# Adding seven experts' results to the residual stream by indirect DMAs instead of products with a 0/1 matrix

## The chip, the cores and the metric

The kernel runs on one core of one Trainium2 chip. The metric is the device time of one execution in microseconds. The kernel before took 1603.03 us in the median of 3 runs (1602.83 to 1605.2). The profile belongs to one further execution of 1603.41 us, whose span from the first to the last instruction is 1601.0 us.

## The reference

The reference is a decoder trunk of two layers on 256 tokens of 1024 channels in float32. Each layer has a token mixer (block-sparse attention and dilated windows, gated and projected) and then a channel mixer. The channel mixer of layer 0 is a dense SwiGLU. That of layer 1 is a top-2-of-8 mixture of experts:

```python
logits = h @ w_router                       # 256 x 8
top_val, top_idx = lax.top_k(logits, 2)
top_w = softmax(top_val)
combine[t, e] = top_w where e is one of the two experts of token t, else 0
for e in range(8):
    y = y + combine[:, e:e+1] * (silu(h @ w_gate[e]) * (h @ w_up[e])) @ w_down[e]
x = rms_norm(x + y)                         # the output
```

An expert has 3584 hidden channels, so its three weight matrices are 44 MB, and all eight are read, whatever the routing.

## The kernel before

**Precision and the weight stream.** Every weight matrix is streamed from device memory in units of 128 x 2048 float32 (1 MB), issued by SyncE (`Stream.load`, L143). A unit is cut into two halves, and each half is split into a high and a low part in the TensorE's float32r form: ScalarE copies (`wh`, L153), VectorE subtracts (`wl`, L154). TensorE then makes three products for every 128 x 512 piece: high weights by high activations (L257), high weights by low activations (L258), low weights by high activations (L262). The splitting runs four halves ahead of the products. In the expert stage fourteen slots (`raw`, `ringa`, `ringb`) hold units; a slot is loaded again when VectorE has finished splitting it.

**The expert stage** (`experts`, `expert_prep`, `down`). The tokens of an expert are collected into 128 slots. `G` is a 0/1 matrix, tokens by slots (`select`, L780). Products of `G` with small per-token columns `rc` give the slot's norm factor, its routing weight and its token number (`scales`, L815). For experts 1 to 7 an indirect DMA on GpSimd's queue gathers the tokens' rows from `xd`, a copy of the residual stream in device memory (`fetch`, L788); `store_x` (L327) writes that copy in two halves. An expert is worked off in seven chunks of 512 hidden channels: gate, up, then the chunk before's down product, which accumulates in two PSUM banks `acc` over all seven chunks. Thus expert e's down product ends in the first chunk of expert e+1.

**The end of an expert** (`down`, L850 to L870). ScalarE scales `acc` by the routing weight into `yh` (L858), and VectorE makes the rest `yl` (L859). `scatter` multiplies both by `GT`, the transpose of `G` (L865 and L866; in the trace yh and yl are parts of a tile called `tmp`), which brings the 128 slots back to 256 token rows, and VectorE adds the product to the residual stream `xo` in SBUF (L868; `xo` lies in a tile called `late`). There are two halves of 512 channels and two halves of the tokens, so four such scatters for an expert. `GT` is made by `trans` (two transposes, L824, and a copy, L826).

**The order of the work.** Each engine's queue is written out by the program. A list of pending steps with due times in modelled TensorE microseconds (`soon`, `later`, `tick`) inserts the small steps between the products; only the large products move that model's clock.

Of the kernel before, what the change touches and what calls it, by code (L numbers as in the profile page):

```python
# [11 lines left out]
F32 = mybir.dt.float32  # L12
# [7 lines left out]
P = 128  # L20
# [151 lines left out]
def trunk(ctx: ExitStack, tc: tile.TileContext, x, xt, wpre, wmoe, cst, cstb, gfin, out):  # L172
# [151 lines left out]
            soon(at + 1, lambda: sumsq(xs, c))  # L324

    def store_x(c):
        nc.gpsimd.dma_start(M["xd"].rearrange("(b p) d -> p b d", p=P)[:, :, c * 512:(c + 1) * 512],  # L327
                            xs[:, :, c * 512:(c + 1) * 512])

    def make_rstd():  # L330
        V.scalar_tensor_tensor(ms, ss[:, :, 0], EPS, ss[:, :, 1], op0=ALU.add, op1=ALU.add)  # L331
# [12 lines left out]
    def mixer(i, gnext, last=False):  # L344
        oo = [[], []]

        def out_unit(kh, c):
            unit((th, tl), oo[c], 4 * kh, 4, 512, kh == 0, kh == 1)

        with tc.tile_pool(name=f"mix{i}", bufs=2) as mp:  # L350
            with tc.tile_pool(name=f"att{i}", bufs=2, side="right", reuse_waits="tile") as ap:
                gates = attention(mp, ap)
            if last:
                moe_ring()
            projections(mp, gates)
            oo[0] += [mm_ps(), mm_ps()]
            out_unit(0, 0)
            oo[1] += [mm_ps(), mm_ps()]
            out_unit(0, 1)
            flush()  # L360
        if last:
            moe_open()
        for c in range(2):
            out_unit(1, c)
            flush()
            add_x(oo[c], c)
            norm_half(gnext, c)
            if c == 0 and last:
                M["xd"] = dram.tile([S, D], F32, name="xd")
                store_x(0)  # L370
                soon(5.0, lambda: logits(0))

# [335 lines left out]
    def route():  # L708
        ep = M["ep"]

        def small(shape, name, dt=F32):
            return ep.tile(shape, dt, name=name, bufs=1)

        lp = M["lp"]
        lo, L, v8 = small([P, 2, 8], "lo"), small([P, 2, 8], "L"), small([P, 2, 8], "v8")
        R = ep.tile([P, 2, P], F32, name="G", tag="G")
        R1, R2 = (R[:, i, :].rearrange("p (b e j) -> p b e j", b=2, e=8) for i in range(2))
        rank = small([P, 2, 8], "rank")
        sel, slot = small([P, 2, 8], "sel", BF16), small([P, 2, 8], "slot")
        d1, z = small([P, 2, 8], "d1"), small([P, 2, 8], "z")  # L720
        rc = small([P, 2, 8, 3], "rc")
        warm(10)
        for b in range(2):
            A.activation(lo[:, b, :], lp[b][:, 8:16], AF.Copy, scale=rstd[:, b:b + 1])
        for b in range(2):
            V.scalar_tensor_tensor(L[:, b, :], lp[b][:, 0:8], rstd[:, b:b + 1], lo[:, b, :],
                                   op0=ALU.mult, op1=ALU.add)

        lt = C[:, C_LT:C_LT + 64].rearrange("p (e j) -> p e j", e=8).unsqueeze(1).to_broadcast([P, 2, 8, 8])
        lj = L.unsqueeze(2).to_broadcast([P, 2, 8, 8])  # L730
        le = L.unsqueeze(3).to_broadcast([P, 2, 8, 8])
        V.tensor_tensor(R2, lj, le, op=ALU.is_equal)
        V.tensor_tensor(R1, lj, le, op=ALU.is_gt)
        V.tensor_tensor(R2, R2, lt, op=ALU.mult)
        V.tensor_tensor(R1, R1, R2, op=ALU.add)
        V.tensor_reduce(rank, R1, axis=AX.X, op=ALU.add)
        V.tensor_scalar(sel, rank, 1.5, None, op0=ALU.is_lt)
        for b in range(2):
            V.tensor_copy(rc[:, b, :, 0], rstd[:, b:b + 1].to_broadcast([P, 8]))
            V.tensor_copy(rc[:, b, :, 2], C[:, C_TOK + b:C_TOK + b + 1].to_broadcast([P, 8]))  # L740

        pp = mm_ps()
        tri, one = CB[:, 0:128], CB[:, 128:256]
        T.matmul(pp[:, 0:8], tri, sel[:, 0, :], start=True, stop=True)
        T.matmul(pp[:, 8:16], one, sel[:, 0, :], start=True, stop=False)
        T.matmul(pp[:, 8:16], tri, sel[:, 1, :], start=False, stop=True)
        T.matmul(pp[:, 16:24], one, sel[:, 0, :], start=True, stop=False)
        T.matmul(pp[:, 16:24], one, sel[:, 1, :], start=False, stop=True)
        V.tensor_tensor(slot, pp[:, 0:16].rearrange("p (b e) -> p b e", b=2), sel, op=ALU.mult)
        M["slot"], M["rc"] = slot, rc  # L750

        def weights():
            most, mosti = small([P, 1], "most"), small([P, 1], "mosti", I32)
            V.tensor_reduce(most, pp[:, 16:24], axis=AX.X, op=ALU.max)
            V.tensor_copy(mosti, most)
            M["most"] = mosti
            for b in range(2):
                V.max(v8[:, b, :], L[:, b, :])

            for b in range(2):  # L760
                V.tensor_scalar(d1[:, b, :], L[:, b, :], -2.0, v8[:, b, 0:1], op0=ALU.mult, op1=ALU.add)
            for b in range(2):
                V.tensor_scalar(z[:, b, :], d1[:, b, :], v8[:, b, 1:2], 88.0, op0=ALU.add, op1=ALU.min)
            nc.gpsimd.tensor_tensor(z, base_e.unsqueeze(2).to_broadcast([P, 2, 8]), z, op=ALU.pow)

        def weights2():
            V.tensor_scalar(z, z, 1.0, None, op0=ALU.add)
            V.reciprocal(z, z)
            V.tensor_tensor(rc[:, :, :, 1], z, sel, op=ALU.mult)
        return weights, weights2  # L770

    def expert_prep(e, off):

# [35 lines left out]

        def scales(c0, c1):  # L810
            if not c0:
                sl["sc"] = ep.tile([P, 2], F32, name="sc", tag="sc")
            p = tp_ps()
            for b in range(2):
                T.matmul(p[:, c0:c1], sl["G"][:, b, :], M["rc"][:, b, e, c0:c1], start=b == 0, stop=b == 1)  # L815
            V.tensor_copy(sl["sc"][:, c0:min(c1, 2)], p[:, c0:min(c1, 2)])
            if c1 > 2:
                sl["idx"] = ep.tile([P, 1], I32, name="idx", tag="idx")
                V.tensor_copy(sl["idx"], p[:, 2:3])

        def trans():
            p = tp_ps()
# [4 lines left out]

        M["slots", e] = sl
        if by_dma:
            return [select, lambda: scales(0, 3), fetch, lambda: gather(0), lambda: gather(1), trans]  # L830
        both = (0, 1, 2) if e == 0 and not off else (0, 2)
        return [select, lambda: gather(0), lambda: gather(1), trans,
                *(lambda c=c: scales(*c) for c in zip(both, both[1:]))]

# [6 lines left out]
                  lambda b, k=k0 + 2 * q + i: tl[:, k, par * P:(par + 1) * P], [out], k0 + 2 * q + i == 0,  # L841
                  k0 + 2 * q + i == 7) for i in range(2)])

    def down(e, j, gT, first):
        ep, sl, xo = M["ep"], M["slots", e], M["xo"]
        if j == 0:
            sl["acc"] = [acc_ps(), acc_ps()]
        for c in range(2):
            acc = sl["acc"][c]
            for q in (0, 2):  # L850
                h, l = W.take()
                run([(h[:, i * 512:(i + 1) * 512], l[:, i * 512:(i + 1) * 512],
                      lambda b, i=q + i: gT[0][:, i, :], lambda b, i=q + i: gT[1][:, i, :], [acc],
                      j == 0 and q + i == 0, j == NCH - 1 and q + i == 3) for i in range(2)])
            if j == NCH - 1:
                yh, yl = M["y"][:, 0], M["y"][:, 1]
                cw = sl["sc"][:, 1:2]
                A.activation(yh, acc, AF.Copy, scale=cw)  # L858
                V.scalar_tensor_tensor(yl, acc, cw, yh.bitcast(F32), op0=ALU.mult, op1=ALU.subtract)  # L859

                assert W.released(M["late"][1])

                def scatter(b, c=c):
                    p = tp_ps()
                    T.matmul(p, sl["GT"][:, b * P:(b + 1) * P], yh, start=True, stop=False)  # L865
                    T.matmul(p, sl["GT"][:, b * P:(b + 1) * P], yl, start=False, stop=True)  # L866
                    s0, s1 = c * 512, (c + 1) * 512
                    V.tensor_tensor(xo[:, b, s0:s1], (xs if first else xo)[:, b, s0:s1], p, op=ALU.add)  # L868
                for b in range(2):
                    soon(PAR[f's{c}'] + PAR[f'sd{c}'] * b, lambda f=scatter, b=b: f(b))  # L870

    def experts(off, first, weights=()):
        ep = M["ep"]
        prep = expert_prep(0, off)
        for fn in prep[:3]:
# [8 lines left out]
        for e in range(NE):  # L884
            for j in range(NCH):
# [23 lines left out]
                    split_ps(gT[0], gT[1], p.rearrange("p (k s) -> p k s", k=4))  # L909
                soon(PAR['gl'] if e == NE - 1 and j == NCH - 1 else PAR['gt'], g_transpose)  # L910
                if prev:
                    down(*prev, first and prev[0] == 0)
                prev = (e, j, gT)
                if j == 2 and e + 1 < NE:
                    for wait, fn in zip((0.0, 2.0, 4.0, 20.0, 22.0, 24.0), expert_prep(e + 1, off)):
                        later(wait, fn)
                if j == NCH - 1:
                    drain()
        down(*prev, False)
        flush()  # L920

    wrhl = base.tile([P, 8, 16], F32R, name="wrhl")
# [39 lines left out]
    make_rstd()  # L962
    store_x(1)
    logits(1)
    experts(0, True, route())

    for c in range(2):
        sumsq(M["xo"], c)
# [6 lines left out]
    with tc.If(most > P):  # L975
        W = Stream(nc, lambda i: wmoe[i], nmoe, hp)
        W.add_slots(ring + M["ring"][:-1])
        experts(P, False)
        for c in range(2):
            sumsq(M["xo"], c)  # L980

# [75 lines left out]
```

## Time and profile before

| | before |
|---|---|
| median of 3 runs | 1603.03 us |
| the profiled execution | 1603.41 us |
| its span | 1601.0 us |
| TensorE busy (products) | 1575.7 us, 98% |
| VectorE busy | 1292.3 us, 81% |
| ScalarE busy | 1093.0 us, 68% |
| moved by DMA | 460.87 MB, 288 GB/s in the mean |

The experts run from about 603 us to 1590 us of the span. The names in a row are tiles (out<-in), the line is that of the code above. TensorE's products are pipelined: the duration shown for one, 0.39 us, is longer than the distance from its start to the next one's start, which is about 0.23 us for a 128 x 512 product. What an instruction costs TensorE is therefore read from the starts of its neighbours and not from its own duration.

### The profile page before, as it was taken

The page shows a single profiled execution, that of the slowest core. Times are in us where ns is not written, and L with a number is a line of the kernel's source. Part 1 is how long each engine was busy: PE and PEld are TensorE (multiplying, and loading weights), DVE is VectorE, ACT ScalarE, POOL GpSimd, SP SyncE. Part 2 cuts the span into 40 slices and gives each one's busy share as a digit, 9 for nine tenths or more (in the row PEclk, how much of TensorE's full clock was granted, in tenths as well). Part 3 has the DMA queues.
Part 4 walks back from the last instruction along what each step waited for, and adds up shares of the span by engine and source line. Part 5 has one row for each costly group of instructions (what it writes and reads, how often), then busy time and mean ns, then how long its engine had stood idle before and what let it go on. Part 6 is the DMA issues. An engine that isn't in the chain of part 4 may idle for free. (4 is left out here: it accounts for less than half of the span.)

```text
span 1601.0 us, 20811 instructions
## 1 busy us (share of the span) xinstructions
PE 1575.7 (98%) x7493; PEld 1284.7 (80%) x7493; DVE 1292.3 (81%) x1663; ACT 1093.0 (68%) x1413; POOL 17.0 (1%) x19
## 2 busy tenths in 40 slices
PE   8999999999999999999999999999999999999996
PEld 6777888888877888888888888888888888888885
DVE  7767665555686678899899899899899899899996
ACT  6556454444556557787787787787787778787784
POOL 0000000000000000000000000000000000000000
PEclk9999999999999999999999999999999999999998
DMA  8444555555444596999999999999999999999970
GB/s 335 171 146 136 184 181 187 183 185 197 165 146 156 195 402 270 358 355 360 369 360 364 367 363 359 373 357 362 371 358 361 355 376 369 350 368 375 360 258 28
DMA packets 65600, 460.87 MB, mean 288 GB/s; under 512 B 7248, under 2 KB 7504, under 8 KB 10704
## 3 DMA queue, kind: packets, MB, share of 16 engines
q1 hardware_dynamic: 64192, 454.73, 76.1%
q0 software_dynamic: 1296, 4.72, 0.9%
q8 instruction: 61, 1.00, 0.2%
q14 instruction: 51, 0.42, 0.1%
HBM read 457.33 MB, written 2.10 MB: 287 GB/s over the span
## 5 line engine op out<-in xcount | busy, mean ns | idle before, releaser
L257 PE MATMUL mm<-wh,th 128*128 128x512 f32 (+1 forms) x1536 | 601.6, 393 | 3.0 <-ACT wh L153 3.0
L258 PE MATMUL mm<-wh,tl 128*128 128x512 f32 (+1 forms) x1536 | 590.3, 386 | 0.0
L154 DVE TENSOR_TENSOR wl<-raw,wh 128x1024 fp32r<-128x1024 f32 x376 | 446.7, 1220 | 135.1 <-ACT wh L153 134.0
L153 ACT ACTIVATE wh<-raw 128x1024 fp32r<-128x1024 f32 x376 | 390.5, 1057 | 148.7 <-PE mm L258 114.4
L262 PE MATMUL mm<-wl,th 128*128 128x512 f32 (+1 forms) x1536 | 452.0, 390 | 0.0
L154 DVE TENSOR_TENSOR wl<-ringa,wh 128x1024 fp32r<-128x1024 f32 x290 | 341.0, 1219 | 36.4 <-ACT wh L153 36.3
L257 PEld LDWEIGHTS mm<-wh,th 128*128 128x128 f32 x1536 | 288.8, 188 | 65.0 <-issue 5.7
L258 PEld LDWEIGHTS mm<-wh,tl 128*128 128x128 f32 x1536 | 289.0, 188 | 54.7
L153 ACT ACTIVATE wh<-ringa 128x1024 fp32r<-128x1024 f32 x290 | 297.7, 1058 | 45.0 <-PE mm L258 27.2
L262 PEld LDWEIGHTS mm<-wl,th 128*128 128x128 f32 x1536 | 279.7, 188 | 55.7 <-issue 2.0
L154 DVE TENSOR_TENSOR wl<-ringb,wh 128x1024 fp32r<-128x1024 f32 x188 | 218.1, 1218 | 15.3 <-ACT wh L153 15.3
L153 ACT ACTIVATE wh<-ringb 128x1024 fp32r<-128x1024 f32 x188 | 192.3, 1068 | 18.0 <-PE acc L258 11.2
L257 PE MATMUL acc<-wh,gT 128*128 128x512 f32 x224 | 87.3, 390 | 0.0
L258 PE MATMUL acc<-wh,gT 128*128 128x512 f32 x224 | 87.2, 389 | 0.0
L258 PE MATMUL acc<-wh,tmp 128*128 128x512 f32 x224 | 87.2, 389 | 0.0
L257 PE MATMUL acc<-wh,tmp 128*128 128x512 f32 x224 | 87.2, 389 | 0.0
L262 PE MATMUL acc<-wl,tmp 128*128 128x512 f32 x224 | 69.1, 390 | 0.0
L262 PE MATMUL acc<-wl,gT 128*128 128x512 f32 x224 | 69.1, 390 | 0.0
L891 ACT ACTIVATE g<-mm,sc 128x512 f32<-128x512 f32 x56 | 38.7, 691 | 39.6 <-PE mm L262 39.6
L262 PEld LDWEIGHTS acc<-wl,gT 128*128 128x128 f32 x224 | 42.0, 188 | 8.8
L258 PEld LDWEIGHTS acc<-wh,gT 128*128 128x128 f32 x224 | 42.0, 188 | 8.8
L262 PEld LDWEIGHTS acc<-wl,tmp 128*128 128x128 f32 x224 | 42.0, 188 | 8.8
(184 smaller groups left out, 1232.7 us busy)
## 6 DMA issues: line engine op xcount, KB each, us to landing
ringa<-in_wmoe_dram SPq DMA_DIRECT2D x144, 1024.0 KB, 7.1
raw<-in_wmoe_dram SPq DMA_DIRECT2D x96, 1024.0 KB, 7.0
ringb<-in_wmoe_dram SPq DMA_DIRECT2D x94, 1024.0 KB, 7.0
raw<-in_wpre_dram SPq DMA_DIRECT2D x91, 1024.0 KB, 4.8
late<-in_wmoe_dram SPq DMA_DIRECT2D x2, 1024.0 KB, 8.0
raw<-in_wpre_dram SPq DMA_DIRECT2D x2, 512.0 KB, 5.8
xs<-in_x_dram SPq DMA_DIRECT2D x2, 512.0 KB, 7.3
ringa<-in_wpre_dram SPq DMA_DIRECT2D x1, 1024.0 KB, 7.0
```

Source lines behind the costliest of these rows:

```text
L153: self.nc.scalar.activation(h, s, AF.Copy)
L154: self.nc.vector.tensor_tensor(l, s, h.bitcast(F32), op=ALU.subtract)
L257: T.matmul(o, xh(b), wh, start=start, stop=False)
L258: T.matmul(o, xl(b), wh, start=False, stop=False)
L262: T.matmul(o, xh(b), wl, start=False, stop=stop)
L891: A.activation(g, og, AF.Silu, scale=sl["sc"][:, 0:1])
```

## The change

A second copy of the residual stream in device memory, `yd`, is written beside `xd`. It has 128 rows more than there are tokens. For experts 0 to 6 the scaled result `y` (128 slots by 1024) is written by ScalarE alone into one half of the buffer `xo` (even experts one half, odd ones the other), and one indirect DMA per expert, issued by GpSimd, adds its 128 rows to the rows of `yd` that `to` names: the token's row, or one of the 128 extra rows where the slot is empty. Three small VectorE instructions per expert work out `to`, for which `rc` has a fourth column of ones. `GT` is no longer made for experts 1 to 6; expert 0 still makes it. The last expert keeps the old way: during its fifth chunk SyncE loads the 256 rows of `yd` into `xo`, and its four scatters are added there. A second pass for experts with more than 128 tokens, which is not taken in the profiled execution, keeps the old way for all.

```diff
     def store_x(c):
-        nc.gpsimd.dma_start(M["xd"].rearrange("(b p) d -> p b d", p=P)[:, :, c * 512:(c + 1) * 512],
-                            xs[:, :, c * 512:(c + 1) * 512])
+        for t in ("xd", "yd"):
+            nc.gpsimd.dma_start(M[t][0:S].rearrange("(b p) d -> p b d", p=P)[:, :, c * 512:(c + 1) * 512],
+                                xs[:, :, c * 512:(c + 1) * 512])
...
                 M["xd"] = dram.tile([S, D], F32, name="xd")
+
+                M["yd"] = dram.tile([S + P, D], F32, name="yd")
                 store_x(0)
...
+        V.memset(rc[:, :, :, 3], 1.0)
+        V.tensor_scalar(dump, C[:, C_TOK + 1:C_TOK + 2], float(P), None, op0=ALU.add)
+        M["dump"] = dump
...
+    def to_dram(e, off):
+
+        return not off and e < NE - 1
...
         def scales(c0, c1):
...
-            V.tensor_copy(sl["sc"][:, c0:min(c1, 2)], p[:, c0:min(c1, 2)])
-            if c1 > 2:
-                sl["idx"] = ep.tile([P, 1], I32, name="idx", tag="idx")
-                V.tensor_copy(sl["idx"], p[:, 2:3])
+            V.tensor_copy(sl["sc"][:, c0:c1], p[:, c0:c1])
+            if c1 == 4:
+
+                sc, dump = sl["sc"], M["dump"]
+                row = ep.tile([P, 1], F32, name="row", tag="row")
+                for n in ("idx", "to"):
+                    sl[n] = ep.tile([P, 1], I32, name=n, tag=n)
+                V.tensor_copy(sl["idx"], sc[:, 2:3])
+                V.scalar_tensor_tensor(row, sc[:, 3:4], dump, sc[:, 2:3], op0=ALU.mult, op1=ALU.subtract)
+                V.tensor_scalar(sl["to"], row, -1.0, dump, op0=ALU.mult, op1=ALU.add)
...
-            return [select, lambda: scales(0, 3), fetch, lambda: gather(0), lambda: gather(1), trans]
+            return [select, lambda: scales(0, 4), fetch, lambda: gather(0), lambda: gather(1), *([] if to_dram(e, off) else [trans])]
...
             if j == NCH - 1:
-                yh, yl = M["y"][:, 0], M["y"][:, 1]
                 cw = sl["sc"][:, 1:2]
+                if to_dram(e, off):
+                    assert W.released(M["late"][1])
+                    y = xo[:, e % 2]
+                    A.activation(y[:, c * 512:(c + 1) * 512], acc, AF.Copy, scale=cw)
+                    if c:
+                        nc.gpsimd.indirect_dma_start(
+                            out=M["yd"], out_offset=bass.IndirectOffsetOnAxis(ap=sl["to"], axis=0), in_=y,
+                            in_offset=None, compute_op=ALU.add)
+                    continue
+                yh, yl = (M["y"][:, t] for t in range(2))
...
-                    V.tensor_tensor(xo[:, b, s0:s1], (xs if first else xo)[:, b, s0:s1], p, op=ALU.add)
+                    V.tensor_tensor(xo[:, b, s0:s1], xo[:, b, s0:s1], p, op=ALU.add)
...
+                if j == 4 and e == NE - 1 and not off:
+                    nc.sync.dma_start(M["xo"], M["yd"][0:S].rearrange("(b p) d -> p b d", p=P))
```

TensorE's queue at the end of an expert's down product (here expert 1, before; `acc` is the down product, `tmp` holds yh and yl, `mm` would be the next expert's gate product):

```order
L262 MATMUL acc<-wl,tmp 128x512 x2
L865 MATMUL tp<-tmp,GT 128x512
L866 MATMUL tp<-tmp,GT 128x512
L257 MATMUL acc<-wh,tmp 128x512
L258 MATMUL acc<-wh,tmp 128x512
L257 MATMUL acc<-wh,tmp 128x512
L258 MATMUL acc<-wh,tmp 128x512
L865 MATMUL tp<-tmp,GT 128x512
L866 MATMUL tp<-tmp,GT 128x512
L262 MATMUL acc<-wl,tmp 128x512 x2
L908 MATMUL tp<-C,g 128x128 x4
```

The same place in the changed kernel:

```order
L262 MATMUL acc<-wl,tmp 128x512 x2
L257 MATMUL acc<-wh,tmp 128x512
L258 MATMUL acc<-wh,tmp 128x512
L257 MATMUL acc<-wh,tmp 128x512
L258 MATMUL acc<-wh,tmp 128x512
L262 MATMUL acc<-wl,tmp 128x512 x2
L931 MATMUL tp<-C,g 128x128 x4
```

The four scatter products of the first half of the channels are gone and nothing has moved into their places; the other four of this expert, further on among the gate products, go in the same way.

GpSimd's queue from the first store on, before:

```order
L327 DMA xd<-xs 128x2x512
L332 TENSOR_TENSOR rstd<-ms,nhalf 128x2
L327 DMA xd<-xs 128x2x512
L764 TENSOR_TENSOR z<-base_e,z 128x16
L788 DMA xg<-xd,idx 128x1024 x7
L974 TENSOR_LOAD mosti
```

and in the changed kernel, up to the second expert's addition:

```order
L328 DMA xd<-xs 128x2x512
L328 DMA yd<-xs 128x2x512
L333 TENSOR_TENSOR rstd<-ms,nhalf 128x2
L328 DMA xd<-xs 128x2x512
L328 DMA yd<-xs 128x2x512
L770 TENSOR_TENSOR z<-base_e,z 128x16
L798 DMA xg<-xd,idx 128x1024
L878 DMA yd<-late_4866,to 384x1024
L798 DMA xg<-xd,idx 128x1024
L878 DMA yd<-late_4866,to 384x1024
```

Each store has a twin, and each gather of tokens (`xg`) is followed by the addition of the expert before it; SyncE's queue gets one load, `late_4866<-yd`, behind its last expert weight.

## Rows read from the trace of the kernel before

**Rows 1.** The page: each engine's busy us; TensorE's granted clock in 40 slices.

```profile
PE 1575.7 (98%) x7493; PEld 1284.7 (80%) x7493; DVE 1292.3 (81%) x1663; ACT 1093.0 (68%) x1413; POOL 17.0 (1%) x19
...
PEclk9999999999999999999999999999999999999998
```

**Rows 2.** Windows: length, busy PE, PEld, DVE, ACT, POOL, clock, DMA share, GB/s.

```profile
560.00:600.00 40.00, 39.63 (x203) 32.34 (x202) 28.39 (x43) 20.51 (x34) 2.39 (x3) 0.98 0.99 401
...
880.00:1000.00 120.00, 118.89 (x543) 97.72 (x543) 109.65 (x114) 94.38 (x107) 1.23 (x1) 1.00 0.97 363
```

**Rows 3.** Waits of TensorE from 640 to 1600 us: total us, times, longest.

```profile
PE tp L815 <- DVE G L780: 6.2, 7, 0.9
PE tp L866 <- DVE tmp L859: 1.9, 8, 0.3
```

**Rows 4.** Waits of SyncE's DMA queue, whole span.

```profile
SPq L143 <- DVE wl L154: 1242.4, 392, 19.3
```

**Rows 5.** TensorE in time, scatters of two experts: start, duration, instruction.

```profile
983.87 0.39 PE L865 MATMUL tp<-tmp,GT 128*128 128x512 f32 x1
984.49 0.50 PE L866 MATMUL tp<-tmp,GT 128*128 128x512 f32 x1 [0.23 <-DVE tmp L859]
984.82 0.40 PE L257 MATMUL acc<-wh,gT 128*128 128x512 f32 x1
...
990.35 0.39 PE L865 MATMUL tp<-tmp,GT 128*128 128x512 f32 x1
...
990.81 0.40 PE L257 MATMUL mm<-wh,th 128*128 128x512 f32 x1
...
1106.70 0.39 PE L865 MATMUL tp<-tmp,GT 128*128 128x512 f32 x1
```

**Rows 6.** TensorE in time, the two transposes that make GT.

```profile
1050.16 0.40 PE L262 MATMUL mm<-wl,th 128*128 128x512 f32 x1
1050.40 0.38 PE L824 MATMUL tp<-C,G 128*128 128x128 f32 x2
...
1050.85 0.39 PE L257 MATMUL mm<-wh,th 128*128 128x512 f32 x1
```

**Rows 7.** Groups by line, 620 to 1600 us: busy us, mean ns, idle before.

```profile
L868 DVE TENSOR_TENSOR late<-late,tp 128x512 f32<-128x512 f32 x28 | 19.0, 681 | 1.9 <-PE tp L866 1.9
...
L859 DVE SCALAR_TENSOR_TENSOR tmp<-acc,sc,tmp 128x512 fp32r<-128x512 f32 x16 | 11.9, 744 | 2.8 <-ACT tmp L858 2.8
```

**Rows 8.** DMA, 880 to 1000 us: a queue's share; median us to landing.

```profile
q0 software_dynamic: 144, 0.52, 1.6%
...
ringa<-in_wmoe_dram SPq DMA_DIRECT2D x18, 1024.0 KB, 7.1
...
xg<-xd,idx POOLq DMA_INDIRECT x1, 10.1
```

**Rows 9.** SyncE's weight loads in time, 1440 to 1601 us.

```profile
1443.83 9.65 SPq L143 DMA_DIRECT2D raw<-in_wmoe_dram  x4
...
1486.07 8.63 SPq L143 DMA_DIRECT2D raw<-in_wmoe_dram  x4
...
1539.55 2.60 SPq L143 DMA_DIRECT2D ringb<-in_wmoe_dram  x2
```

**Rows 10.** VectorE in time, at the routing and at an expert's scales.

```profile
602.82 0.17 DVE L749 TENSOR_TENSOR slot<-mm,sel 128x16 f32<-128x16 f32 x1 [1.59 <-PE mm L748]
...
1028.25 1.23 DVE L154 TENSOR_TENSOR wl<-ringa,wh 128x1024 fp32r<-128x1024 f32 x1 [0.73 <-ACT wh L153]
```

**Rows 11.** GpSimd in time, 590 to 640 us.

```profile
597.82 0.71 POOL L332 TENSOR_TENSOR rstd<-ms,nhalf 128x2 f32<-128x2 f32 x1 [9.50 <-DVE ms L331]
598.49 0.77 POOL L327 DMA_DIRECT2D xd<-xs  x1
```

**Rows 12.** ScalarE ending expert 6; VectorE's first addition of expert 7.

```profile
1479.15 0.69 ACT L858 ACTIVATE tmp<-acc,sc 128x512 fp32r<-128x512 f32 x1
...
1585.22 0.69 DVE L868 TENSOR_TENSOR late<-late,tp 128x512 f32<-128x512 f32 x1 [0.59 <-PE tp L866]
```

More of the change, by code (lines that the diff above doesn't have):

```diff
@@ L720, in route @@
         d1, z = small([P, 2, 8], "d1"), small([P, 2, 8], "z")
-        rc = small([P, 2, 8, 3], "rc")
+        rc, dump = small([P, 2, 8, 4], "rc"), small([P, 1], "dump")
         warm(10)
@@ L811, in scales @@
             if not c0:
-                sl["sc"] = ep.tile([P, 2], F32, name="sc", tag="sc")
+                sl["sc"] = ep.tile([P, 4], F32, name="sc", tag="sc")
             p = tp_ps()
@@ L829, in expert_prep @@
         if by_dma:
-            return [select, lambda: scales(0, 3), fetch, lambda: gather(0), lambda: gather(1), trans]
-        both = (0, 1, 2) if e == 0 and not off else (0, 2)
+            return [select, lambda: scales(0, 4), fetch, lambda: gather(0), lambda: gather(1), *([] if to_dram(e, off) else [trans])]
+        both = (0, 1, 4) if not off else (0, 4)
         return [select, lambda: gather(0), lambda: gather(1), trans,
@@ L842, in expert_unit, with down @@
                   k0 + 2 * q + i == 7) for i in range(2)])
-    def down(e, j, gT, first):
+    def down(e, j, gT, off):
         ep, sl, xo = M["ep"], M["slots", e], M["xo"]
@@ L855, in down @@
             if j == NCH - 1:
-                yh, yl = M["y"][:, 0], M["y"][:, 1]
                 cw = sl["sc"][:, 1:2]
+                if to_dram(e, off):
[8 more added lines that the diff above has]
+                yh, yl = (M["y"][:, t] for t in range(2))
                 A.activation(yh, acc, AF.Copy, scale=cw)
                 V.scalar_tensor_tensor(yl, acc, cw, yh.bitcast(F32), op0=ALU.mult, op1=ALU.subtract)
-                assert W.released(M["late"][1])
                 def scatter(b, c=c):
@@ L867, in scatter, with experts @@
                     s0, s1 = c * 512, (c + 1) * 512
-                    V.tensor_tensor(xo[:, b, s0:s1], (xs if first else xo)[:, b, s0:s1], p, op=ALU.add)
+                    V.tensor_tensor(xo[:, b, s0:s1], xo[:, b, s0:s1], p, op=ALU.add)
                 for b in range(2):
                     soon(PAR[f's{c}'] + PAR[f'sd{c}'] * b, lambda f=scatter, b=b: f(b))
-    def experts(off, first, weights=()):
+    def experts(off, weights=()):
         ep = M["ep"]
@@ L911, in experts @@
                 if prev:
-                    down(*prev, first and prev[0] == 0)
+                    down(*prev, off)
                 prev = (e, j, gT)
+                if j == 4 and e == NE - 1 and not off:
+                    nc.sync.dma_start(M["xo"], M["yd"][0:S].rearrange("(b p) d -> p b d", p=P))
                 if j == 2 and e + 1 < NE:
@@ L918, in experts @@
                     drain()
-        down(*prev, False)
+        down(*prev, off)
         flush()
@@ L964, in trunk @@
     logits(1)
-    experts(0, True, route())
+    experts(0, route())
     for c in range(2):
@@ L977, in trunk @@
         W.add_slots(ring + M["ring"][:-1])
-        experts(P, False)
+        experts(P)
         for c in range(2):
```

## The prediction, made before the changed kernel had run

> **What bounds the kernel now.** I read the page first, for who is busy. TensorE works through 98% of the span, at its upper clock level of 2.4 GHz in nearly every slice [rows 1]. VectorE and ScalarE are well below it. The windows come next, because an average over stages can hide a second limit. In the expert stage, which the change touches, TensorE is busy 118.89 of 120 us, VectorE 109.65, ScalarE 94.38, and the DMA engines show a share of 0.97 at 363 GB/s [rows 2]. So three resources are near the top, and the question is which ends last. The waits answer it. TensorE's only waits of any size are two small ones on VectorE, at the scales (6.2 us in 7 times) and at the scatter (1.9 us in 8 times); none is on a DMA [rows 3]. SyncE, which issues the weights, waits for slots that VectorE has to free, 1242.4 us in all [rows 4]: the stream is ahead of its users. TensorE's own list of instructions is the bound, and an instruction taken from it shortens the span by the distance it takes up between its neighbours' starts, as long as nothing else then becomes last.
>
> **What goes from TensorE.** In expert 2 the first scatter begins at 983.87 and the next ordinary product at 984.82: 0.95 us, of which the yl part makes TensorE wait [rows 5]. A later one goes from 990.35 to 990.81: 0.46 us [rows 5]. An expert has one of the first kind and three of the second, 0.95 + 3 x 0.46 = 2.33 us, and seven experts lose them: 16.3 us. The two transposes for GT: after the L262 at 1050.16 a second L262 and then L257 would follow at 0.23 us each, at 1050.62; L257 starts at 1050.85 [rows 6]. That is 0.23 us, for the six experts 1 to 6: 1.4 us. Together 17.7 us. From one expert to the next TensorE takes 1106.70 - 983.87 = 122.83 us [rows 5], and would take 122.83 - 2.33 - 0.23 = 120.27 us. The order shows nothing added to TensorE but one column in a product of a few columns.
>
> **VectorE and ScalarE.** Per expert VectorE loses two yl of 0.744 us and four additions of 0.681 us [rows 7], 4.2 us. It gains two tiny instructions, of the size of the 0.17 us of the slot product [rows 10], and the four there now depend on each other: I take 0.5 us. At that place it then waits 0.73 us for ScalarE [rows 10], and the split weights are four halves ahead, so this costs nothing; without the cover 7 x 0.5 = 3.5 us. The memset and `dump` at the routing stand ahead of a wait of 1.59 us for TensorE [rows 10]: nothing, or 0.3 us uncovered. ScalarE scales the same two halves as before, 0.69 us each [rows 12], and is rid of the copy of GT. Its new wait, for the buffer that the expert two before used, ends about two periods after that DMA was issued.
>
> **GpSimd and SyncE.** The store's twin takes an issue of 0.77 us; the first pair lies in the 9.50 us that GpSimd idles ahead of `rstd`, the second behind `rstd` [rows 11]. Uncovered it would be 0.8 us on the routing's path. The addition waits for ScalarE's second half and for the addition before it, one period back; behind it in the queue stands the next gather of tokens, due two chunks later (a chunk is 122.83 / 7 = 17.5 us). The load of `yd` stands behind SyncE's last expert weight, issued by about 1542 [rows 9]. It waits for expert 6's addition, issued at about 1480, and is first used at 1585.22 [rows 12]. So the addition has some 60 us before it holds up SyncE, behind which only the final norm's gain waits, and the load has 43 us for 1 MB, where a weight unit lands in 7.1 [rows 8]. Nothing.
>
> **The addition itself.** This is the cost that the trace does not show: 0.52 MB per expert that is read in SBUF and in device memory and written back. Its bounds, in microseconds Y for which it keeps the 16 engines from the weights: a gather of as many bytes takes 1.6% of 120 us, 1.9 us, when they move once [rows 8], and that is the low end; it can't be below nothing, since bytes are only added. At the high end, reading and writing each hold all engines for a gather's whole landing of 10.1 us [rows 8]: 20.2 us. I take 4 us, twice the gather's busy time, because the gather is the row with the same rows and sizes.
>
> What is there to hide it: an expert's weights and gather, 44.56 MB, take 111.1 us at the 401 GB/s that the engines reached between 560 and 600 us [rows 2]. In a period of 120.27 us that leaves 9.2 us. Beside it, a slot's reload comes 1486.07 - 1443.83 = 42.2 us before the next, for fourteen loads [rows 9]; a unit lands in 7.1 us [rows 8] and is split within about 3 (a fourteenth), so the stream can fall behind by 32 us in all before TensorE waits. The loss is then 7 x (Y - 9.2) - 32: it begins at Y = 13.8. At 4 us it is nothing.
>
> The windows show 363 GB/s held over an expert, and 401 GB/s for 40 us [rows 2]. The Trainium skill, in "DMA: Bandwidth & Descriptors", section "Bandwidth", puts the limit of device memory at about 358 GB/s per core, which would make the weights the bound already. By that figure 45.6 MB would take 127.4 us, 7 x 7.1 = 50 us too long less the 32 of the ring, so an estimate of 1603, no change. The trace exceeds that figure in both windows; the section itself gives single-core numbers above it, with the pair's other core idle.
>
> **Sum.** 1603.41 - 17.7 = 1585.7 us for the profiled execution; its time is 0.4 above the median of the runs, so 1585.5, and a span of 1583.3.
>
> **The rivals.**
> - The weight stream is the bound. For it: a share of 0.97. Against: SyncE's waits, and 401 GB/s at a share of 0.99. If 363 were the limit, 45.6 MB (the addition counted as read and written) take 125.6 us, 5.3 over the new period; 7 x 5.3 - 32 = 5 us given back: 1590.5.
> - Slower: the additions hold the DMA engines. Each is a row-wise read, add and write, and no row shows how fast that goes beside a full stream. It outweighs the gain of 17.7 when 7 x (Y - 9.2) - 32 exceeds it, from Y = 16.3 us. At the high end of 20.2 the loss is 45 us: 1630. It would show as ScalarE's splits waiting for weights, from about the fifth expert on. Against: the gather of the same rows delays nothing.
> - No change: the same with Y near 16.
> - More: VectorE, relieved of 4.2 us, is early at the scales too and the 6.2 us there go [rows 3]: 1579. Against: the scales come two chunks later, where VectorE already keeps pace with ScalarE.
> That VectorE would become the bound is out: 109.65 of 120 us falls.
>
> **How the numbers follow.** The forecast of 1585.5, with a range of its own of 1583 to 1588, gets 0.84. The stream as the bound, or an addition between 13.8 and 16 us, gets 0.05, no change 0.03, slower 0.05, more 0.03. A difference of 0.2%, 3.2 us, is about what can be told from no change. Faster is 0.84 + 0.05 + 0.03 = 0.92, the same 0.03, slower 0.05. The range runs from 1582 to 1592, which takes in the uncovered 3.5 us and 0.8 us and the stream's 1590.5, and leaves out the slow cases and the far end of the fast one.
>
> **What would show it.** Right: TensorE's period from expert to expert at 120.3 us, no wait of TensorE or ScalarE on a weight, landings still near 7 us, the scales' wait unchanged near 0.9 us each. Wrong: landings of weights that grow from expert to expert (the addition's price), a period above 121 us, a wait of VectorE's last additions on the load of `yd`, or a longer gap of TensorE at the routing.

## The result, and the profile after

The changed kernel took 1585.97 us in the median of 4 runs (1584.43 to 1589.62), the kernel before 1602.93 in 4 runs beside it: a ratio of 0.9896, 95% interval 0.9884 to 0.9908. Forecast were 1585.5 us and a range of 1582 to 1592. The profiled execution took 1585.93 us with a span of 1584.2.

The page of the changed kernel: busy us of each engine, and what device memory moved. The second fence is the same line of the page before:

```profile
PE 1560.4 (99%) x7425; PEld 1273.7 (80%) x7425; DVE 1269.5 (80%) x1640; ACT 1090.5 (69%) x1407; POOL 32.2 (2%) x28
...
HBM read 458.38 MB, written 6.82 MB: 294 GB/s over the span
```

```profile
HBM read 457.33 MB, written 2.10 MB: 287 GB/s over the span
```

TensorE has 68 products fewer than in [rows 1]: 7 x 8 scatters and 6 x 2 transposes. The written bytes grew by 4.72 MB, which are the second copy (1.05) and seven additions of 0.524.

One expert of the changed kernel in the windows (columns as in [rows 2]):

```profile
860.00:980.00 120.00, 119.14 (x545) 98.31 (x544) 108.89 (x113) 95.89 (x109) 3.20 (x2) 1.00 0.99 376
```

TensorE stays as full as before, the others are little changed, and the DMA engines move 376 GB/s where it was 363 [rows 2]: the same weights in a shorter time, and the addition.

The waits of TensorE from 640 to 1590 us, which answer to [rows 3]:

```profile
PE tp L825 <- DVE G L790: 6.0, 7, 0.9
PE tp L888 <- ACT tmp L883: 0.8, 1, 0.8
PE tp L889 <- DVE tmp L884: 0.3, 1, 0.3
```

The scales' wait stayed (6.0 us for 6.2). The yl wait is that of the last expert alone. The first wait of its scatter, 0.8 us for ScalarE, was there before too; nothing new has come.

TensorE at the end of expert 1, the place of the first order in the section on the change; scatters like those of expert 2 in [rows 5] are missing, and L931 follows L262 without a gap:

```profile
858.41 0.62 PE L262 MATMUL acc<-wl,tmp 128*128 128x512 f32 x2
858.86 0.39 PE L257 MATMUL acc<-wh,tmp 128*128 128x512 f32 x1
...
859.77 0.62 PE L262 MATMUL acc<-wl,tmp 128*128 128x512 f32 x2
860.23 0.60 PE L931 MATMUL tp<-C,g 128*128 128x128 f32 x4
```

Where the time went is read from a mark that every expert has, the issue of the gather of the next tokens on GpSimd. The first store, and the first and the last of the seven gathers, before:

```profile
587.37 0.95 POOL L327 DMA_DIRECT2D xd<-xs  x1 [181.63 <-DVE xs L341]
...
658.75 1.27 POOL L788 DMA_INDIRECT xg<-xd,idx  x1 [35.09 <-PE mm L258]
...
1395.58 1.23 POOL L788 DMA_INDIRECT xg<-xd,idx  x1 [121.59 <-DVE idx L819]
```

and GpSimd in the changed kernel, from the first store on:

```profile
587.85 0.95 POOL L328 DMA_DIRECT2D xd<-xs  x1 [181.63 <-DVE xs L342]
588.80 0.77 POOL L328 DMA_DIRECT2D yd<-xs  x1
598.30 0.71 POOL L333 TENSOR_TENSOR rstd<-ms,nhalf 128x2 f32<-128x2 f32 x1 [8.73 <-DVE ms L332]
...
659.40 1.63 POOL L798 DMA_INDIRECT xg<-xd,idx  x1 [35.24 <-PE mm L258]
742.07 1.65 POOL L878 DMA_INDIRECT yd<-late,to  x1 [81.04 <-ACT late L876]
...
1380.81 1.61 POOL L798 DMA_INDIRECT xg<-xd,idx  x1 [35.94 <-PE mm L258]
1463.80 1.59 POOL L878 DMA_INDIRECT yd<-late,to  x1 [81.38 <-ACT late L876]
```

Six periods took 736.83 us before and take 721.41 now: 122.81 and 120.24 us for one, 2.57 less, 15.4 in six. From the last gather to the end of the span it was 205.42 and is 203.39: 2.0 less, where the seventh scatter is gone. (Up to TensorE's last product, 193.59 and 191.20 us, it is 2.4 less; the rest lies behind it, in the final norm.) The start up to the first gather came 0.65 us later. 15.4 + 2.0 - 0.65 = 16.8, the difference of the spans, 1601.0 and 1584.2.

The DMA from 860 to 880 us of the changed kernel, where expert 1's addition runs (queue, packets, MB, share; then KB each and us to landing):

```profile
q0 software_dynamic: 144, 0.52, 14.0%
raw<-in_wmoe_dram SPq DMA_DIRECT2D x4, 1024.0 KB, 8.9
...
yd<-late,to POOLq DMA_INDIRECT x1, 11.2
```

An addition takes 14.0% of 20 us, 2.8 us of the 16 engines, and lands in 11.2 us. The weights beside it land in 8.9 us instead of 7.1 [rows 8], and from 870 to 900 us, with the end of the addition in them, the engines reach 416 GB/s:

```profile
DMA packets 1732, 12.47 MB, mean 416 GB/s; under 512 B 196, under 2 KB 196, under 8 KB 225
```

SyncE's load of `yd` went out behind the last weights without waiting:

```profile
1522.34 2.60 SPq L143 DMA_DIRECT2D ringb<-in_wmoe_dram  x2
1525.13 0.38 SPq L938 DMA_DIRECT2D late<-yd  x1
```

It landed in 8.8 us, and the first addition that reads it began at 1568.07.

### The profile page after: what moved, and what is told of

Read it like the earlier page. It is cut to its first block, busy times and chain, and to the rows that moved or that the text cites. A ratio compares the mean times of both kernels' runs of the same rounds, so it can differ in the third digit from the quotient of the medians.

```text
span 1584.2 us, 20697 instructions
## 1 busy us (share of the span) xinstructions
PE 1560.4 (99%) x7425; PEld 1273.7 (80%) x7425; DVE 1269.5 (80%) x1640; ACT 1090.5 (69%) x1407; POOL 32.2 (2%) x28
## 3 DMA queue, kind: packets, MB, share of 16 engines
HBM read 458.38 MB, written 6.82 MB: 294 GB/s over the span
## 5 line engine op out<-in xcount | busy, mean ns | idle before, releaser
L262 PE MATMUL mm<-wl,th 128*128 128x512 f32 (+1 forms) x1536 | 450.1, 389 | 0.0
L262 PEld LDWEIGHTS mm<-wl,th 128*128 128x128 f32 x1536 | 279.7, 188 | 56.5 <-issue 2.0
L154 DVE TENSOR_TENSOR wl<-ringb,wh 128x1024 fp32r<-128x1024 f32 x188 | 218.2, 1219 | 15.4 <-ACT wh L153 15.4
L262 PE MATMUL acc<-wl,tmp 128*128 128x512 f32 x224 | 69.1, 389 | 0.0
L262 PE MATMUL acc<-wl,gT 128*128 128x512 f32 x224 | 69.0, 389 | 0.0
L258 PEld LDWEIGHTS acc<-wh,tmp 128*128 128x128 f32 x224 | 42.1, 188 | 8.8
L262 PEld LDWEIGHTS acc<-wl,gT 128*128 128x128 f32 x224 | 42.0, 188 | 8.7
L262 PEld LDWEIGHTS acc<-wl,tmp 128*128 128x128 f32 x224 | 42.0, 188 | 8.7
```

The source lines that it names most:

```text
L154: self.nc.vector.tensor_tensor(l, s, h.bitcast(F32), op=ALU.subtract)
L258: T.matmul(o, xl(b), wh, start=False, stop=False)
L262: T.matmul(o, xh(b), wl, start=False, stop=stop)
```

## The experiments

The theory is the prediction's: TensorE's list is the bound, what was taken from it is the gain, and the addition is hidden. Its rivals are that the gain came from VectorE's relief, and that the addition costs something on the path. The times of one kernel's runs lie 2 to 5 us apart, so the period between gathers, which agrees to 0.05 us among traces, carries the small differences. All edits are to the changed kernel.

**The changed kernel again**, as a control.

> The changed kernel as it is, beside the experiments on the same chip. Every theory: 1586 us, 17 us below the kernel before, and 120.25 us from one addition's issue to the next one's.

1586.7 us (1585.05 to 1588.04), ratio 0.9901 (0.9885 to 0.9916). Gathers at 658.44 and 1379.82: a period of 120.23 us. The mark repeats.

**Without the additions.**

```diff
-                    if c:
-                        nc.gpsimd.indirect_dma_start(
-                            out=M["yd"], out_offset=bass.IndirectOffsetOnAxis(ap=sl["to"], axis=0), in_=y,
-                            in_offset=None, compute_op=ALU.add)
```

> The seven additions are left out (the results of experts 0 to 6 don't reach the output); all else stays. Theory (the additions are hidden behind TensorE): the same time as the changed kernel within 1 us, 1586, the period of 120.25 us unchanged; only the landings of the weights near the end of an expert go back to about 7 us. Rival (the additions take something from the path through DMA or GpSimd): faster, by up to their 3 us of DMA time per expert, 21 us: 1565.

```profile
659.51 1.62 POOL L798 DMA_INDIRECT xg<-xd,idx  x1 [35.26 <-PE mm L258]
...
1380.89 1.58 POOL L798 DMA_INDIRECT xg<-xd,idx  x1 [118.67 <-PE mm L258]
```

These two lines are its first and last gather: a period of 120.23 us, the same. The time was 1583.81 us (ratio 0.988, 0.9865 to 0.9895), 2.9 below the control in the median, where 1 us was expected. The intervals overlap and the profiled span, 1584.1, is that of the changed kernel; what made the unprofiled runs shorter is not settled, but it is not in the periods. The next run but one, which makes all additions, has as low a median (1583.94). The rival's 21 us are excluded. The weights land in 7.4 us from 860 to 880 us, where they took 8.9 beside the addition.

**Products put back into TensorE's list.**

```diff
+                    def idle_products():
+                        p = tp_ps()
+                        for t in range(2):
+                            T.matmul(p, th[:, 0, 0:P], th[:, 0:2, :], start=t == 0, stop=t == 1)
+                    for b in range(2):
+                        soon(PAR[f's{c}'] + PAR[f'sd{c}'] * b, idle_products)
```

> Eight 128x512 products per expert are put back into TensorE's queue at the places of the old scatter, for experts 0 to 6. They read the next activations, wait for nothing on VectorE and nobody reads them. Theory (TensorE's own list is the bound): 7 x 8 x 0.2275 = 12.7 us slower than the changed kernel, 1598.7, period 122.1 us; the old scatter's other 3.6 us were its wait for yl. Rival (the gain came from VectorE's relief of 4.2 us per expert): less than 4 us slower, 1590 at most.

```profile
657.68 1.63 POOL L798 DMA_INDIRECT xg<-xd,idx  x1 [35.24 <-PE mm L258]
...
1390.02 1.61 POOL L798 DMA_INDIRECT xg<-xd,idx  x1 [36.85 <-PE mm L258]
```

The gathers of this kernel give a period of 122.06 us, 1.82 above the control's 120.23, or 0.228 for each of the eight products. The time was 1597.54 us (0.9965, 0.9953 to 0.9977), 10.8 above the control (12.0 in the profiled spans, 12.7 expected). The products alone bring back seven tenths of the 2.57 us. What is left to the kernel before, 122.81 - 122.06 = 0.75 us, is put down to GT and the wait for yl; the next run but one tests GT.

**VectorE's work put back.**

```diff
+                    V.scalar_tensor_tensor(M["y"][:, 1], acc, cw, y[:, c * 512:(c + 1) * 512],
+                                           op0=ALU.mult, op1=ALU.subtract)
+                    def idle_add(b, c=c):
+                        s0, s1 = c * 512, (c + 1) * 512
+                        V.tensor_tensor(M["y"][:, 0], xs[:, b, s0:s1], xs[:, b, s0:s1], op=ALU.add)
+                    for b in range(2):
+                        soon(PAR[f's{c}'] + PAR[f'sd{c}'] * b, lambda b=b: idle_add(b))
```

> VectorE's old work at an expert's end is put back for experts 0 to 6: two yl and four additions of 128x512 per expert at the old places, on data that nobody uses; TensorE's list stays that of the changed kernel. Theory: nothing, 1586 within 1 us, period 120.25 us, since no product waits for it. Rival (VectorE's relief is a part of the gain): 1589 to 1600, with TensorE waiting at the scales for longer than 0.9 us.

```profile
657.40 1.63 POOL L798 DMA_INDIRECT xg<-xd,idx  x1 [35.24 <-PE mm L258]
...
1378.81 1.61 POOL L798 DMA_INDIRECT xg<-xd,idx  x1 [35.44 <-PE mm L258]
```

The work is there: from 860 to 980 us VectorE is busy 112.19 us (the fourth number), 3.3 more than in the changed kernel:

```profile
860.00:980.00 120.00, 119.14 (x544) 98.30 (x544) 112.19 (x119) 95.90 (x109) 3.69 (x2) 1.00 0.99 376
```

The period is 120.24 us, and the time 1583.94 (0.9888, 0.9872 to 0.9903), not above the control. TensorE's wait at the scales is 6.0 us as before. VectorE's relief was worth nothing; that rival falls.

**GT, four times.**

```diff
-            return [select, lambda: scales(0, 4), fetch, lambda: gather(0), lambda: gather(1), *([] if to_dram(e, off) else [trans])]
+            return [select, lambda: scales(0, 4), fetch, lambda: gather(0), lambda: gather(1), trans, *([trans] * 3 if to_dram(e, off) else [])]
-                    for wait, fn in zip((0.0, 2.0, 4.0, 20.0, 22.0, 24.0), expert_prep(e + 1, off)):
+                    for wait, fn in zip((0.0, 2.0, 4.0, 20.0, 22.0, 24.0, 26.0, 28.0, 30.0), expert_prep(e + 1, off)):
```

> The transposes that make GT, with ScalarE's copy, are put back for experts 1 to 6 and done four times at four places. Theory: 6 x 4 x 0.23 = 5.5 us slower than the changed kernel, 1591.5, period 121.2 us. Rival (a pair of transposes fits into gaps that TensorE has anyway): nothing, 1586.

```profile
658.99 1.63 POOL L798 DMA_INDIRECT xg<-xd,idx  x1 [35.24 <-PE mm L258]
...
1386.43 1.61 POOL L798 DMA_INDIRECT xg<-xd,idx  x1 [35.94 <-PE mm L258]
```

A period of 121.24 us, 1.01 above the control: 0.25 us for a pair of transposes. The time was 1590.76 us (0.9914, 0.9899 to 0.993), 4.1 above the control, and the profiled span 5.9 above its span; 6 x 1.01 = 6.1 stand in the periods. So of the 0.75 us left above, 0.25 are GT. The other 0.50 are a remainder: no run put the wait for yl back by itself, and anything else of the change would stand in it too. The starts in [rows 5] give that wait 0.95 - 0.46 = 0.49 us, which fills it.

**Four additions for one.** Three go into further tensors.

```diff
+                M["more"] = [dram.tile([S + P, D], F32, name=f"more{i}") for i in range(3)]
...
-                        nc.gpsimd.indirect_dma_start(
-                            out=M["yd"], out_offset=bass.IndirectOffsetOnAxis(ap=sl["to"], axis=0), in_=y,
+                        for dst in [M["yd"], *M["more"]]:
+                            nc.gpsimd.indirect_dma_start(
+                                out=dst, out_offset=bass.IndirectOffsetOnAxis(ap=sl["to"], axis=0), in_=y,
```

> Each addition is done four times, three of them into further tensors in device memory that nobody reads. One addition took about 3 us of the 16 engines in the changed kernel's trace (10.1% of 30 us), so Y = 12. Theory by the prediction's formula, 7 x (Y - 9.2) - 32, which begins at Y = 13.8: nothing, 1586, but landings of the weights that grow. Rival (the additions hold the engines for longer than their share shows, the 11 us of their landing): Y = 44, so some 210 us slower.

The same 20 us of the DMA as above:

```profile
q0 software_dynamic: 377, 1.41, 35.8%
raw<-in_wmoe_dram SPq DMA_DIRECT2D x4, 1024.0 KB, 15.7
```

The weights land in 15.7 us, and TensorE notices nothing:

```profile
659.71 1.61 POOL L799 DMA_INDIRECT xg<-xd,idx  x1 [35.28 <-PE mm L258]
...
1381.06 1.60 POOL L799 DMA_INDIRECT xg<-xd,idx  x1 [28.05 <-PE mm L258]
```

That is a period of 120.23 us; the time was 1586.89 us (0.989, 0.9874 to 0.9905). The engines had room for three additions more.

**Eight.** The same edit with seven further tensors.

> Each addition is done eight times, seven of them into tensors that nobody reads: Y = 24. Theory by the formula with 401 GB/s: 7 x (24 - 9.2) - 32 = 72 us slower, 1658; with the 416 GB/s that the changed kernel reached between 870 and 900 us, the free time is 13.1 us and the loss 44 us, 1630. Rival (the ring and the engines take eight too): 1586.

1623.98 us (1.012, 1.0104 to 1.0136), 37 above the control, in the direction of the theory and by another way. Its second period is already 128 us, ScalarE never waits for a weight, and the new waits are VectorE's:

```profile
778.49 1.00 POOL L799 DMA_INDIRECT xg<-xd,idx  x1 [17.95 <-PE mm L258]
...
906.48 1.00 POOL L799 DMA_INDIRECT xg<-xd,idx  x1 [17.95 <-PE mm L258]
```

```profile
DVE to L836 <- DMA more<-late,to: 46.4, 5, 10.1
DVE to L836 <- DMA xg<-xd,idx: 9.7, 1, 9.7
```

The tile `to` has two buffers. The row numbers of the expert after next go into the buffer that the additions, issued two chunks earlier, still read. So VectorE stood still for up to 10 us, with the splitting behind it. This wait was in the changed kernel's order too, and the prediction didn't list it: an addition that lands in 11 us is long done there.

**Eight and twelve, with four buffers for the row numbers.**

```diff
-                    sl[n] = ep.tile([P, 1], I32, name=n, tag=n)
+                    sl[n] = ep.tile([P, 1], I32, name=n, tag=n, bufs=4)
```

> As the kernel with eight additions, but the tiles with the row numbers (idx and to) have four buffers each, so that VectorE doesn't wait for the additions of the expert before when it writes the next row numbers (46.4 us in 5 times there). By the shares of that trace eight additions take about 21 us of the engines. Theory (the rest of the limit is the DMA engines' time, and the ring of slots lends 32 us): weights and gather 107.1 us at 416 GB/s and 21 make 128, 8 us over the period of 120.25; 7 x 8 - 32 = 24 us slower than the changed kernel, 1610, with the first four periods at 120.25 us and ScalarE waiting for weights in the last ones. Rival (VectorE's wait was all of it): 1586, all periods at 120.25.

1614.11 us (1.0074, 1.0057 to 1.009), 27 above the control where 24 were expected. The waits from 1000 to 1560 us name the weights; from 640 to 1000 there is none on a DMA:

```profile
ACT wh L153 <- DMA ringa<-in_wmoe_dram: 21.3, 15, 3.0
ACT wh L153 <- DMA ringb<-in_wmoe_dram: 11.3, 6, 3.0
ACT wh L153 <- DMA raw<-in_wmoe_dram: 9.0, 6, 3.1
```

Its windows show an expert before the ring was used up, and one after:

```profile
860.00:980.00 120.00, 119.14 (x545) 98.30 (x544) 108.88 (x113) 95.90 (x109) 21.34 (x9) 1.00 1.02 384
...
1100.00:1220.00 120.00, 109.11 (x480) 88.62 (x479) 96.57 (x102) 84.55 (x96) 21.34 (x9) 0.96 1.02 384
```

The gathers at 657.26, 777.43, 897.67 and 1018.24 give periods of 120.2, 120.2 and 120.6; then come 131.1, 123.4 and 130.8. ScalarE's waits begin at 1015 us, and TensorE first waits for a weight's split part at 1130.59, 390 us after the first addition. What the weights' queue moved in these 390 us, and in as long from the changed kernel's first addition (packets, MB, share):

```profile
q1 hardware_dynamic: 17982, 130.97, 81.5%
...
q1 hardware_dynamic: 19676, 143.31, 94.0%
```

The stream was 12.3 MB behind by then, about 30 us at 416 GB/s, and no product had waited for a weight: the fourteen slots lent about the 32 us of the prediction's bound. Most of what TensorE then loses stands in one line, at the scales, where VectorE's list has fallen behind with the splitting:

```profile
PE tp L826 <- DVE G L791: 21.6, 7, 8.6
...
1150.00:1160.00 10.00, 10.00 (x38) 8.05 (x37) 5.91 (x6) 6.46 (x7) 1.41 (x1) 0.81 1.01 422
```

The line was 6.0 us in the changed kernel. Behind its longest wait, 8.6 us, the granted clock was 0.81 in the 10 us shown, which is partly the lower level of 1.2 GHz: 38 products started there, and 48 in the next 10 us. So a part of the 27 us is the clock, which the 24 expected did not hold: about 2 us after this wait, an estimate from the ten products at some 0.21 us each.

> Twelve additions per expert, row numbers in four buffers. About 31 us of the engines. Theory: 107.1 + 31 = 138 us, 18 over the period; 7 x 18 - 32 = 94 us slower than the changed kernel, 1680, the ring used up after about two experts. Rival (weights and additions overlap in the engines, shares over 1 were seen): below 1630.

1683.64 us (1.0506, 1.0488 to 1.0523), 97 above the control, 94 expected; but the number agrees and the way does not. The periods are even, about 137 us from the second on, and what TensorE waits for is the gather of tokens:

```profile
PE tp L807 <- DMA xg<-xd,idx: 83.1, 6, 14.4
```

The gather stands behind twelve additions in the same DMA queue and lands in 31.7 us (median; 6.0 in the changed kernel), past its use 18 us after its issue. So this run does not test the ring.

**A version that is faster than both.** TensorE's wait at the scales was in both kernels. The products with the scales are moved back by 1.4 us of the order's model, the gather's issue by 0.8, and expert 0's unused GT goes.

```diff
-        return [select, lambda: gather(0), lambda: gather(1), trans,
+        return [select, lambda: gather(0), lambda: gather(1), trans if not to_dram(e, off) else (lambda: None),
...
-                    for wait, fn in zip((0.0, 2.0, 4.0, 20.0, 22.0, 24.0), expert_prep(e + 1, off)):
+                    for wait, fn in zip((0.0, 3.4, 4.8, 20.0, 22.0, 24.0), expert_prep(e + 1, off)):
```

> A version meant to be faster than both. The products with the scales stand 1.4 us (modelled) further behind the making of G in TensorE's queue, and expert 0's GT, which the changed kernel makes and doesn't use, is left out. Theory: TensorE's wait at the scales (6.0 us in 7 times, about 1.0 us each between the neighbours' starts) goes, and 0.23 us with GT: 7 us faster than the changed kernel, 1579, period 119.2 us. Rival (VectorE's queue makes the scales late wherever they stand): 1586.

1576.23 us (0.983, 0.9817 to 0.9844), 10.5 below the control. The waits of TensorE from 640 to 1590 us:

```profile
PE tp L888 <- ACT tmp L883: 0.8, 1, 0.8
PE tp L889 <- DVE tmp L884: 0.3, 1, 0.3
```

Only the last expert's are left.

```profile
657.97 1.63 POOL L798 DMA_INDIRECT xg<-xd,idx  x1 [36.12 <-DVE to L835]
...
1372.58 1.71 POOL L798 DMA_INDIRECT xg<-xd,idx  x1 [37.07 <-PE mm L262]
```

These gathers give 119.10 us, 1.13 less than the control's: seven times that is 7.9 us. Expert 0's GT adds 0.25 at the price found above, and the rest of the 10.5 lies outside the periods, within the scatter of runs. The wait had stood in the list with 0.86 us each, and its end gave 1.13.

## Why the prediction was right, point by point

- **What bounds.** Shown. The products put back cost their full distance, VectorE's work put back nothing.
- **TensorE's savings.** 2.33 us for the scatters and 0.23 for GT were read from the starts of the neighbours, 2.56 together. The period fell by 2.57, to 120.24 us, forecast 120.27. Put back by themselves, the products cost 1.82 and GT 0.25. The 0.50 that remain agree with the 0.49 read for the wait for yl, but no run tested that part alone. The list of waits has it at 0.23 each [rows 5], so it understates the price. Durations would have misled: eight scatter products of 0.39 us are 3.1 us.
- **The sum.** 17.7 us were forecast and 16.8 came in the profiled spans. The start up to the first gather, where nothing was taken away, came 0.65 us later, and 0.48 of that already stands at the first store, ahead of its twin (587.37 and 587.85). The first gather lies between 656.4 and 659.7 us in the other traces, so most of it is scatter; the twin store shows no cost. GpSimd's idle time ahead of `rstd` shrank from 9.50 [rows 11] to 8.73, by the twin's 0.77, as the cover was reckoned.
- **VectorE and ScalarE.** VectorE lost 3.1 us per period (109.65 and 108.89 of 120 us, times 122.81 and 120.24), a little less than the 3.7 reckoned, and it did not matter. `row` and `to` take 0.21 us each, not 0.17.
- **The addition.** The term that the trace before did not show. Taken were 4 us of the engines, between bounds of 1.9 and 20.2; it is 2.8 us, nearer to the gather than to twice the gather. The free time in a period was put at 9.2 us by 401 GB/s; the engines reach 416, so it was 13.1. Both errors were on the safe side. The onset of a loss at Y = 13.8 (Y is the time that an expert's additions take of the engines) is bracketed: four additions (some 8 to 11 us) lose nothing, eight (21 us) lose 27 us. The formula with 9.2 us would have had 51 for eight, with 13.1 it gives about the 24 expected. The weights beside an addition landed in 8.4 to 9.0 us for experts 0 to 5 and in 9.9 for expert 6, where the prediction's sign was near 7; they did not grow from expert to expert.
- **The stream as the bound.** It was not: 376 GB/s over an expert now, and no wait on a weight. The Trainium skill's figure of 358 GB/s for device memory per core ("DMA: Bandwidth & Descriptors", "Bandwidth") is passed over an expert, with the kernel on one core; the measurement decides. The same section calls its own higher numbers single-core ones and gives about 358 for a core when both cores of a pair stream. No run here loads a second core.
- **The slower rival.** Its mechanism exists, as the run with eight additions and free row numbers shows, seven additions away from this kernel. Missing from the list was a nearer one, VectorE's wait for the buffer of row numbers.
- **The faster rival.** VectorE's relief did not take the scales' wait away. Moving the products behind it did.

## What to carry to other kernels

When one engine's list is full and its few waits are known, a saving can be read from the starts of the neighbours, here to a few hundredths of a microsecond in the period, and a run with idle instructions put back tests it. A DMA whose price no trace shows is bounded by two things that it shows: the rate the engines have reached elsewhere and the time by which the loads run ahead. When an indirect DMA reads a small tile of row numbers, count that tile's buffers among the waits: in this kernel it came free only when the DMA had landed.

## What the runs showed of the hardware that was not expected

- An addition of 128 rows of 4 KB into device memory took 2.8 us of the 16 DMA engines and landed in 11.2 us beside a weight stream. Of four in a row the three further ones landed in 15.9 us (median over the run), of eight the seven further ones in 20.5 and 21.3 in the two runs.
- The reading half of the additions is not in the page's count of bytes read: read grew by 1.05 MB, the load of `yd`, and by nothing from no additions to eight for each expert (458.38 MB in each), while written went from 3.15 to 32.51 MB.
- GpSimd's issue of a gather took 1.23 us before and 1.6 us in the changed kernel, with the same rows, and also without the additions; with eight additions most took 1.00. Why was not tried.
- Busy shares of the DMA engines over 1 (1.02 with eight additions) go with 384 GB/s, less than the 416 at other times, so in these rows the share does not tell how much room is left.
